# Weight sums for the up projection's Strassen pairs, made in DRAM by accumulating transfers during the mixer

## The chip, the cores and the metric

The kernel runs on one core of one Trainium2 chip. The metric is device time of one execution in microseconds (us), lower is better. Before the change, three runs took 1665.97, 1667.84 and 1670.0 us; the median is 1667.84 us. The engines are TensorE (PE, its weight loads PEld), VectorE (DVE), ScalarE (ACT), GpSimd (POOL) and SyncE (SP). SP and ACT issue nearly all transfers before the change. Each engine works through its own instructions in order and waits for others by semaphores.

## What is computed

One decoder layer on 1024 tokens of width 1024: a mixer (S5 and mLSTM branches, merged by gates), cross-attention into 256 memory tokens, and a gated feed-forward part with a causal convolution over three tokens. What the change touches is the last of these:

```python
def _conv_ffn(h, w_up, conv_w, conv_b, w_down):
    u = _causal_dwconv(h @ w_up, conv_w, conv_b)
    a, b = jnp.split(u, 2, axis=-1)
    return (jax.nn.gelu(a) * b) @ w_down
```

The weight `w_up` is 1024 x 5632 and `h` is 1024 x 1024, all float32.

## The kernel before

**Numbers and tiles.** Weights and activations are split into a high part (float32r) and a low one (the rest), and each product is three matmuls: high by high, high by low, low by high. A tile of a projection (`ntile`, L204) loads 512 KB of weights into a WR buffer from SP, ACT casts them to WH (L176), DVE subtracts to make WL (L177), PE runs 48 matmuls into a PSUM tile M (L202), and DVE drains M. The mixer and the attention consist mainly of such tiles, one after the other, with the small work of the S5 and mLSTM branches between them. The list `ORDER` sets the order of the mixer's parts.

**POOL in the mixer.** It does little: it clears buffers in the S5 part (MEMSET, L484), and it computes powers for normalisations, by `G.tensor_tensor(..., op=ALU.pow)`: L775 for each of the four mLSTM heads (tile `dc`), L230 for the vectors `rm` and `r`. DVE prepares `dc` (L774), POOL takes the power (L775), DVE goes on with it (L776, L779), and then PE transposes the scaled head (L782). L776 stands in DVE's queue behind L774 or a few rows later, so DVE waits there until POOL is done.

**The up projection.** The 44 column blocks of `w_up` form 22 pairs f (`NF` = 22; block f of a with block f of b). Each pair is a 2x2 block product by Winograd's form of Strassen's scheme, with seven products p = 1 to 7 in place of eight. In DRAM, `w_up[f]` is 128 x 2048: quarters 0 to 3 hold a11, a12, a21 and a22, 128 x 512 (256 KB) each. The seven weight operands are a11, a12, a22 and four sums s1 to s4, made by `Pair.load` with four DVE instructions (L1129 to L1132):

```python
V.tensor_tensor(out=s1, in0=a21, in1=a22, op=ALU.add)
V.tensor_tensor(out=s2, in0=s1, in1=a11, op=ALU.subtract)
V.tensor_tensor(out=s3, in0=a11, in1=a21, op=ALU.subtract)
V.tensor_tensor(out=s4, in0=a12, in1=s2, op=ALU.subtract)
```

`Pair.weights(p)` splits one operand into high and low; `Pair.product(p)` (matmuls at L1161) runs 12 matmuls for it and adds the PSUM result to the running sums (L1174, L1178). `Pair.conv` (L1184) applies the convolution, `Pair.finish` the gelu and the product, and sends the result to DRAM (`Gd`).

The list `jobs` sets the order. The first eight pairs (f below `NE` = 8, the early pairs) run their products 1 and 2 during the end of the attention, since these need only the first half of the tokens, and keep the sum (pairs 4 to 7 by way of DRAM, `Cd`). Then come products 6, 7, 5, 4, 3 of pairs 0 to 7, and all seven products of pairs 8 to 21. `weights(k + 7)` is called seven jobs ahead. An early pair's `r0` (a11 and a12) is loaded twice, first for products 1 and 2, and again for the sums.

**Buffers and queues.** The 18 Y buffers (128 x 520) hold quarters, sums and split operands; S, R, Z and VV are buffers of 1024 columns. A transfer into a buffer waits until its last reader is done. SP issues the loads of weights, in order. The scheduler decides the order of each engine's instructions at build time.

Of the kernel before, what the change touches and what calls it, by code (L numbers as in the profile page):

```python
# [19 lines left out]
P = 128  # L20
T = 1024
# [10 lines left out]
NF = DFF // P  # L32
# [51 lines left out]
def hybrid_layer(ctx: ExitStack, tc: tile.TileContext, a):  # L86
    nc = tc.nc
    cp = ctx.enter_context(tc.tile_pool(name="cp", bufs=1))
# [17 lines left out]
    def Z(dt=F32):  # L106
        return sp.tile([P, T], dt, tag="Z", bufs=NZ, name=nm("Z"))

    def Y(dt=F32):
        return Yw(dt)[:, :512]  # L110

    def Yw(dt=F32):
        return sp.tile([P, 520], dt, tag="Y", bufs=NY, name=nm("Y"))
# [4 lines left out]
    def psM():  # L118
        return pm.tile([P, T], F32, tag="M", bufs=2, name=nm("M"))

    def psA():
        return pm.tile([P, 512], F32, tag="A", bufs=4, name=nm("A"))
# [4 lines left out]
    V, A, G, PE = nc.vector, nc.scalar, nc.gpsimd, nc.tensor  # L127
# [6 lines left out]
    def col(name, i=0, n=1):  # L134
        o, _ = COLS[name]
        return cols[:, o + i : o + i + n]
# [22 lines left out]
    pw_ = psA()  # L159
    for _ in range(NWARM):  # L160
        PE.matmul(pw_[:, :P], warm, warm, start=True, stop=True)
# [20 lines left out]
    def load_w(src, shape, alloc=None):  # L182
        fw = shape[0] * shape[1]
        raw = wp.tile([P, T], F32, tag="WR", name=nm("WR"))[:, :fw]
        nc.sync.dma_start(out=raw.rearrange("p (k n) -> p k n", k=shape[0]), in_=src)
        if alloc is None:
            hi = wp.tile([P, T], F32R, tag="WH", name=nm("WH"))[:, :fw]
            lo = wp.tile([P, T], F32R, tag="WL", name=nm("WL"))[:, :fw]
        else:
            hi, lo = alloc(F32R)[:, :fw], alloc(F32R)[:, :fw]  # L190
        wcount[0] += 1
        split(hi, lo, raw, low[wcount[0] % 2])
        return (hi.rearrange("p (k n) -> p k n", k=shape[0]),
                lo.rearrange("p (k n) -> p k n", k=shape[0]))

    def gemm_part(ps, wk, xh, xl, width, first, last):

        wh, wl = wk
        spans = [(s, min(s + 512, width)) for s in range(0, width, 512)]
        for lhsT, rhs, is_first, is_last in ((wh, xh, True, False), (wh, xl, False, False), (wl, xh, False, True)):  # L200
            for s, e in spans:
                PE.matmul(ps[:, s:e], lhsT, rhs[:, s:e], start=first and is_first, stop=last and is_last)  # L202

    def ntile(src, xs, nk=KD, width=T):  # L204

        wh, wl = load_w(src, (nk, P))
        ps = psM()
        for k in range(nk):
            gemm_part(ps, (wh[:, k, :], wl[:, k, :]), xs[k][0], xs[k][1], width, k == 0, k == nk - 1)
        return ps  # L210


    def rstd_col(sq, n, out, more=(), alloc=None):
# [57 lines left out]
    for k in range(KD):  # L271
# [6 lines left out]
        for p_ in parts:  # L278
            w = slice(p_[0].start, p_[-1].stop)
# [4 lines left out]
        for p_ in parts:  # L284
            for w_, x_, f, l in ((wh, xh, True, False), (wh, xl, False, False), (wl, xh, False, True)):
                for j in range(3):
                    for h in p_:
                        PE.matmul(pus[j][h.start // 512], w_[:, 0, j * P : (j + 1) * P], x_[:, h],  # L288
                                  start=k == 0 and f, stop=k == KD - 1 and l)
    r1 = cp.tile([P, 8], F32, name="r1")  # L290
# [125 lines left out]
    for w in (1, 2, 4):  # L416
# [30 lines left out]
                      in_=zt[:, : 4 * 7 * CHG].rearrange("p (x k) -> p x k", x=4))  # L447
# [384 lines left out]
    for step in ORDER:  # L832
        i = int(step[1])
# [23 lines left out]
    for j in range(4):  # L857
        ps = ntile(a["w_glu"][j], ysp, nk=4)
# [52 lines left out]
    for i in range(2):  # L911
# [3 lines left out]
        for k4 in range(4):  # L915
            w = slice(k4 * NM, (k4 + 1) * NM)
# [122 lines left out]
    Gd = dr.tile([NF, P, T], F32, name="Gd")  # L1039
    Cd = dr.tile([4, P, T], F32, name="Cd")  # L1040
    H = H0, H1 = slice(0, 512), slice(512, T)
    r3 = cp.tile([P, 8], F32, name="r3")
    x2sq = Z()
    low[:] = [V, V]
# [12 lines left out]
    def o_tile(half, n):  # L1057
        hs = H[half]
        wh, wl = ow.pop(0)
        ps = psA() if half else psM()[:, H0]  # L1060
        for k in range(KD):
            gemm_part(ps, (wh[:, k, :], wl[:, k, :]), oT[k][0][:, hs], oT[k][1][:, hs], 512, k == 0, k == KD - 1)
        xj = x1[n][:, hs]
        V.tensor_tensor(out=xj, in0=xj, in1=ps, op=ALU.add)
        if n == 0:
            A.activation(out=x2sq[:, hs], in_=xj, func=AF.Square)
        else:
            t = Z()[:, H0]
            A.activation(out=t, in_=xj, func=AF.Square)
            V.tensor_tensor(out=x2sq[:, hs], in0=x2sq[:, hs], in1=t, op=ALU.add)  # L1070
        A.dma_start(out=X2d[n][:, hs], in_=xj)

    def o_norm(half):

        rc = r3[:, 4 * half : 4 * half + 4]
        rstd_col([x2sq[:, H[half]]], D, rc, alloc=psM)
        pb = psM()[:, H0]
# [3 lines left out]
    def normed(n, half, pb):  # L1081
        xj = x1[n][:, H[half]]
        V.scalar_tensor_tensor(out=xj, in0=xj, scalar=col("f_g", n), in1=pb, op0=ALU.mult, op1=ALU.mult)
        return xj
# [5 lines left out]
    def put(p, i, f, alloc):  # L1090
        t = alloc(F32R)
        X[p][i] = hi, lo = t[:, H0], t[:, H1]
        split(hi, lo, f)


    NE, HOLD = 8, 4
    wslot = [6]

    class Pair:
# [9 lines left out]
        def load(self, both):  # L1109

            r0 = wp.tile([P, T], F32, tag="WR", name=nm("WR"))
            nc.sync.dma_start(out=r0, in_=a["w_up"][self.f, :, :T])
            a11, a12 = r0[:, H0], r0[:, H1]
            self.src = {1: a11, 2: a12}
            if not both:
                return
            if HOLD <= self.f < NE:
                self.ra = Z()
                nc.sync.dma_start(out=self.ra, in_=Cd[self.f - HOLD])
            if self.f < NE:  # L1120
                a21, a22 = Y(), Y()
                for i, t in enumerate((a21, a22)):
                    nc.sync.dma_start(out=t, in_=a["w_up"][self.f, :, T + 512 * i : T + 512 * i + 512])
            else:
                r1 = S()
                nc.sync.dma_start(out=r1, in_=a["w_up"][self.f, :, T:])
                a21, a22 = r1[:, H0], r1[:, H1]
            s1, s2, s3, s4 = [Y() for _ in range(4)]
            V.tensor_tensor(out=s1, in0=a21, in1=a22, op=ALU.add)  # L1129
            V.tensor_tensor(out=s2, in0=s1, in1=a11, op=ALU.subtract)  # L1130
            V.tensor_tensor(out=s3, in0=a11, in1=a21, op=ALU.subtract)
            V.tensor_tensor(out=s4, in0=a12, in1=s2, op=ALU.subtract)  # L1132
            self.src = {1: a11, 2: a12, 3: s4, 4: a22, 5: s1, 6: s2, 7: s3}

        def weights(self, p):
# [43 lines left out]

        def conv(self, raw, ct):  # L1180
            acc = S()
            A.activation(out=acc, in_=raw, func=AF.Identity, scale=col("fcw", 3 * ct + 2), bias=col("fcb", ct))  # L1182
            for d_ in range(1, 3):
                V.scalar_tensor_tensor(out=acc[:, d_:], in0=raw[:, : T - d_], scalar=col("fcw", 3 * ct + 2 - d_),  # L1184
                                       in1=acc[:, d_:], op0=ALU.mult, op1=ALU.add)
            return acc

# [94 lines left out]
    t2s = []  # L1282
    for i in range(4):
        xe, xo = x1[2 * i], x1[2 * i + 1]
        b12, b22 = normed(2 * i, 1, pb), normed(2 * i + 1, 1, pb)
        V.tensor_tensor(out=xe[:, H0], in0=b12, in1=xe[:, H0], op=ALU.subtract)
        t2 = Y()
        V.tensor_tensor(out=t2, in0=b22, in1=xe[:, H0], op=ALU.subtract)
        put(6, i, t2, S)
        t2s.append(t2)  # L1290
    for k in range(2 * NE, 2 * NE + 2):
        weights(k)
    for i in range(4):
        xe, xo = x1[2 * i], x1[2 * i + 1]
# [5 lines left out]
        weights(k)  # L1300
    for i in range(4):
        xo = x1[2 * i + 1]
        V.tensor_tensor(out=xo[:, H0], in0=xo[:, H0], in1=t2s[i], op=ALU.subtract)
        put(4, i, xo[:, H0], S)
    for i in range(4):
        put(3, i, x1[2 * i + 1][:, H1], S)
# [25 lines left out]
    last = list(range(NF - 2 * FCH, NF))  # L1332
# [146 lines left out]
def build(shapes):  # L1479
    import concourse.bacc as bacc  # L1480

    nc = bacc.Bacc("TRN2", target_bir_lowering=False, num_devices=1, dynamic_dma_scratch_size=2048)
    a = {}
    for n, s in shapes.items():
        a[n] = nc.dram_tensor(f"in_{n}_dram", s, F32, kind="ExternalInput").ap()
    a["out"] = nc.dram_tensor("out_0_dram", (KD, P, T), F32, kind="ExternalOutput").ap()
    with tile.TileContext(nc, schedule_with_timeline_sim=True) as tc:
        hybrid_layer(tc, a)
    return nc
# [11 lines left out]
```

## Time and profile before

| | before |
|---|---|
| median of three runs | 1667.84 us |
| the profiled execution's span | 1665.3 us |
| TensorE busy in it | 1641.3 us |
| VectorE busy in it | 1102.3 us |
| ScalarE busy in it | 664.2 us |
| GpSimd busy in it | 40.1 us, 50 instructions |
| granted TensorE clock, mean | 0.996 |
| HBM read and written | 130.76 MB, 30.93 MB |

The span of the profiled execution goes from its first to its last instruction. A group of instructions in the profile has the source line, the engine, the operation, the tiles that it writes and reads (without the buffer's number), the count, the total busy time, the mean of one in ns, and the idle time ahead of them with what ended it. The chain is the work that ended last, followed back from the end. The matmuls of the up projection (L1161) start at 975.6 us and end at 1411 us; the mixer lies before some 716 us, the attention between them.

### The profile page before, as it was taken

What the parts mean: (1) busy time and instruction counts of PE and PEld (TensorE: products, weight loads), DVE (VectorE), ACT (ScalarE), POOL (GpSimd) and SP (SyncE); (2) the same over time, 40 slices, a digit from 0 to 9 for tenths busy, and PEclk for the clock granted to TensorE, in tenths of its full rate; (3) what the DMA queues carried; (4) which work ended last, traced back from release to release, by engine and by line L of the source; (5) the groups of instructions that cost most, each with busy time, mean ns of one, the idle gap of its engine ahead of it and who ended that gap; (6) DMA issues with size and microseconds to landing.
All of it is one profiled execution on the core that took longest, in us unless ns stands there. A gap on an engine that the chain in (4) does not pass through costs nothing.

```text
span 1665.3 us, 20759 instructions
## 1 busy us (share of the span) xinstructions
PE 1641.3 (99%) x8139; PEld 1373.8 (82%) x8139; DVE 1102.3 (66%) x1752; ACT 664.2 (40%) x1057; POOL 40.1 (2%) x50
## 2 busy tenths in 40 slices
PE   9999999999999999999999999999999999999997
PEld 7897888888888888888888887877888888888887
DVE  7768767675344344523476569999878977976645
ACT  6446544533332223422354336444444444312113
POOL 0000000000000000000000000000000000000014
PEclk9999999999999999999999999999999999999998
DMA  6231411213211133323133345422222226631102
GB/s 194 91 95 43 118 60 58 53 52 92 73 51 51 45 127 128 126 88 101 64 138 116 108 138 190 135 76 101 89 77 89 89 89 244 210 106 59 52 0 102
DMA packets 62851, 163.04 MB, mean 98 GB/s; under 512 B 6881, under 2 KB 20897, under 8 KB 62753
## 3 DMA queue, kind: packets, MB, share of 16 engines
q1 hardware_dynamic: 55216, 143.19, 26.0%
q10 hardware_dynamic: 7536, 18.53, 3.2%
q8 instruction: 64, 1.05, 0.3%
q14 instruction: 35, 0.28, 0.0%
HBM read 130.76 MB, written 30.93 MB: 97 GB/s over the span
## 4 chain that ended last, share of the span: by engine, by line
PE 84%; DVE 8%; DMA 3%; issue 2%; ACT 2%; SPq 0%; POOL 0%; POOLq 0%; DVEq 0%; ACTq 0%
PE M L202 40%; PE A L1161 9%; PE M L1161 8%; PE M L1328 6%; PE A L1328 6%; PE A L202 3%; PE A L1034 1%; DVE S L1184 1%; PE M L288 1%; DMA Y<-in_w_up_dram 1%; PE A L980 1%; PE A L954 1%; DMA WR<-in_w_up_dram 1%; DVE S L177 1%; DVE W L177 1%
## 5 line engine op out<-in xcount | busy, mean ns | idle before, releaser
L202 PE MATMUL M<-S,WH 128*128 128x512 f32 (+1 forms) x1704 | 460.6, 383 | 1.9 <-DVE R L789 1.4
L202 PEld LDWEIGHTS M<-S,WH 128*128 128x128 f32 x1704 | 314.3, 189 | 63.4 <-issue 2.0
L176 ACT CAST WH<-WR 128x1024 fp32r<-128x1024 f32 (+2 forms) x117 | 109.9, 941 | 426.8 <-PE M L202 258.2
L202 PE MATMUL M<-S,WL 128*128 128x512 f32 (+1 forms) x884 | 278.5, 382 | 0.0
L202 PEld LDWEIGHTS M<-S,WL 128*128 128x128 f32 x884 | 166.4, 189 | 31.4
L177 DVE TENSOR_TENSOR WL<-WR,WH 128x1024 fp32r<-128x1024 f32 (+2 forms) x117 | 126.8, 1084 | 81.2 <-ACT WH L176 76.3
L1161 PE MATMUL M<-S,Y 128*128 128x512 f32 x468 | 115.0, 394 | 0.1
L1161 PEld LDWEIGHTS M<-S,Y 128*128 128x128 f32 x468 | 87.7, 188 | 21.1 <-ACT Y L176 0.6
L1184 DVE SCALAR_TENSOR_TENSOR S<-Z,cols,S 128x1023 f32<-128x1023 f32 (+1 forms) x72 | 90.9, 1280 | 3.7 <-ACT S L1182 3.6
L1161 PE MATMUL M<-S,W 128*128 128x512 f32 x324 | 79.1, 391 | 1.0 <-DVE S L1174 1.0
L789 DVE TENSOR_TENSOR R<-M,R 128x1024 f32<-128x1024 f32 x16 | 19.6, 1222 | 84.0 <-PE M L202 84.0
L1161 PEld LDWEIGHTS M<-S,W 128*128 128x128 f32 x324 | 60.6, 188 | 14.8 <-DVE S L1174 1.4
L1161 PE MATMUL A<-S,W 128*128 128x512 f32 x288 | 70.8, 391 | 1.5 <-ACT W L176 1.5
L176 ACT CAST W<-Y 128x512 fp32r<-128x512 f32 x51 | 31.4, 619 | 89.2 <-PE A L1161 67.1
L1161 PEld LDWEIGHTS A<-S,W 128*128 128x128 f32 x288 | 53.9, 188 | 14.0 <-ACT W L176 2.3
L1161 PE MATMUL A<-S,Y 128*128 128x512 f32 x240 | 61.0, 394 | 0.0
L1161 PE MATMUL A<-R,W 128*128 128x512 f32 x228 | 56.4, 391 | 0.0
L1161 PE MATMUL A<-VV,W 128*128 128x512 f32 x216 | 54.7, 395 | 0.0
L1161 PEld LDWEIGHTS A<-S,Y 128*128 128x128 f32 x240 | 45.1, 188 | 10.6
L202 PE MATMUL A<-S,WH 128*128 128x512 f32 (+1 forms) x184 | 53.1, 371 | 0.5 <-ACT WH L176 0.5
L1161 PEld LDWEIGHTS A<-R,W 128*128 128x128 f32 x228 | 42.7, 188 | 9.4 <-ACT Z L1168 0.2
L1182 ACT ACTIVATE S<-Z,cols 128x1024 f32<-128x1024 f32 x36 | 43.2, 1238 | 15.9 <-DVE Z L1178 13.4
(463 smaller groups left out, 3032.2 us busy)
## 6 DMA issues: line engine op xcount, KB each, us to landing
WR<-in_w_up_dram SPq DMA_DIRECT2D x30, 512.0 KB, 3.9
WR<-in_w_in_dram SPq DMA_DIRECT2D x29, 512.0 KB, 3.4
Gd<-S SPq DMA_DIRECT2D x22, 512.0 KB, 2.7
WR<-in_w_down_dram SPq DMA_DIRECT2D x22, 512.0 KB, 3.4
Z<-Gd SPq DMA_DIRECT2D x20, 512.0 KB, 5.2
WR<-in_w_o_dram SPq DMA_DIRECT2D x16, 512.0 KB, 3.4
S<-in_w_up_dram SPq DMA_DIRECT2D x14, 512.0 KB, 3.8
Y<-Rd SPq DMA_DIRECT2D x16, 256.0 KB, 5.2
```

The lines of the kernel that those rows point to most:

```text
L176: A.copy(out=hi, in_=src)
L177: (lo_eng or V).tensor_tensor(out=lo, in0=src, in1=hi.bitcast(F32), op=ALU.subtract)
L202: PE.matmul(ps[:, s:e], lhsT, rhs[:, s:e], start=first and is_first, stop=last and is_last)
L288: PE.matmul(pus[j][h.start // 512], w_[:, 0, j * P : (j + 1) * P], x_[:, h], start=k == 0 and f, stop=k == KD - 1 and l)
L789: V.tensor_tensor(out=gt, in0=ps, in1=rb, op=ALU.mult)
L954: PE.matmul(pv[2 * m + j], lhsT, rhs[:, 0, 512 * j : 512 * j + 512], start=k == 0 and f, stop=k == KD - 1 and l)
L980: PE.matmul(ps[:, i * NM : (i + 1) * NM], lhsT[:, tok], rhs, start=f, stop=l)
L1034: PE.matmul(po, lhsT[:, ns], rhs, start=f, stop=l)
L1161: PE.matmul(ps, lhsT[:, c], rhs, start=f, stop=l, skip_group_check=True)
L1182: A.activation(out=acc, in_=raw, func=AF.Identity, scale=col("fcw", 3 * ct + 2), bias=col("fcb", ct))
L1184: V.scalar_tensor_tensor(out=acc[:, d_:], in0=raw[:, : T - d_], scalar=col("fcw", 3 * ct + 2 - d_), in1=acc[:, d_:], op0=ALU.mult, op1=ALU ...
L1328: PE.matmul(ps[h], lhsT[:, 0, cs_], rhs[:, w], start=f, stop=l)
```

## The change

**New in the mixer.** A DRAM tile `Ws` of 22 x 4 x 128 x 512 (23 MB) holds the four sums of each pair. Each call of `ntile` ends with a call of `up_sums`. After the 2nd, 8th, 14th and so on to the 62nd tile, 11 times, it issues a batch for two pairs from POOL's queue: four copies from `w_up` to `Ws`, the first of which waits for the tile's last matmul, and four accumulating transfers, which add a quarter or another sum to what stands in `Ws`. Each transfer is 512 KB (two pairs, 256 KB each). An accumulate waits for the landing of those that it builds on.

**Only additions.** The four sums are now q2+q3, q0+q2+q3, q0+q2 and q0+q1+q2+q3. The signs that this turns are taken up in the sums of activations (L1286, L1288, L1303) and in the second half's convolution weights (`nfcw`, the negative of the weights in `cols`).

**In the up projection.** `Pair.load` no longer computes sums. It loads s2, s3, s1 and s4 from `Ws` and a22 from `w_up` into five Y buffers. The quarter a21 isn't loaded any more. `r0` is still loaded a second time for the early pairs, with no reader.

```diff
-                PE.matmul(ps[:, s:e], lhsT, rhs[:, s:e], start=first and is_first, stop=last and is_last)
+                last_mm[0] = PE.matmul(ps[:, s:e], lhsT, rhs[:, s:e], start=first and is_first, stop=last and is_last)
...
+SUM_FROM, SUM_STEP = 2, 6
...
+        up_sums()
         return ps
+
+    Ws = dr.tile([NF, 4, P, 512], F32, name="Ws")
+    SB = 2
+    tiles_done = [0]
+
+    def up_sums():
+        tiles_done[0] += 1
+        b, off = divmod(tiles_done[0] - SUM_FROM, SUM_STEP)
+        if off or not 0 <= b < NF // SB:
+            return
+        fs = slice(SB * b, SB * b + SB)
...
+        for i, q in ((0, 2), (1, 0), (2, 0), (3, 1)):
+            d = nc.gpsimd.dma_start(out=o(i), in_=w(q))
+            tc.add_manual_dep(d.ins, last_mm[0].ins.name, DependencyInfo(DependencyClass.Sync, DependencyReason.DATA), reason="pace")
+        nc.gpsimd.dma_start(out=o(0), in_=w(3), accum_op=ALU.add)
+        nc.gpsimd.dma_start(out=o(1), in_=w(2), accum_op=ALU.add)
+        nc.gpsimd.dma_start(out=o(2), in_=o(0), accum_op=ALU.add)
+        nc.gpsimd.dma_start(out=o(3), in_=o(2), accum_op=ALU.add)
...
+    nfcw = cp.tile([P, 3 * NF], F32, name="nfcw")
+    V.tensor_scalar_mul(nfcw, col("fcw", 3 * NF, 3 * NF), -1.0)
...
-            if self.f < NE:
-                a21, a22 = Y(), Y()
-                for i, t in enumerate((a21, a22)):
-                    nc.sync.dma_start(out=t, in_=a["w_up"][self.f, :, T + 512 * i : T + 512 * i + 512])
-            else:
-                r1 = S()
-                nc.sync.dma_start(out=r1, in_=a["w_up"][self.f, :, T:])
-                a21, a22 = r1[:, H0], r1[:, H1]
-            s1, s2, s3, s4 = [Y() for _ in range(4)]
-            V.tensor_tensor(out=s1, in0=a21, in1=a22, op=ALU.add)
-            V.tensor_tensor(out=s2, in0=s1, in1=a11, op=ALU.subtract)
-            V.tensor_tensor(out=s3, in0=a11, in1=a21, op=ALU.subtract)
-            V.tensor_tensor(out=s4, in0=a12, in1=s2, op=ALU.subtract)
+            a22, s1, s2, s3, s4 = [Y() for _ in range(5)]
+            for t, i in ((s2, 2), (s3, 1), (s1, 0), (s4, 3)):
+                nc.sync.dma_start(out=t, in_=Ws[self.f, i])
+                if i == 0:
+                    nc.sync.dma_start(out=a22, in_=a["w_up"][self.f, :, T + 512 :])
```

**Where POOL's instructions stand.** POOL's queue around the powers of heads 1, 2 and 3, before (L775 is the power on `dc`, one row for each head; L484 clears a buffer of the S5 part; the brackets name the engines whose semaphores a row waits for):

```order
L775 TENSOR_TENSOR dc_2205<-dc_2205,mhalf 128x8 [waits DVE_49]
L775 TENSOR_TENSOR dc_2528<-dc_2528,mhalf 128x8 [waits DVE_49,Activation_49,Pool_49]
L484 MEMSET Y_2622 128x256 [waits DVE_49,PE_49]
L775 TENSOR_TENSOR dc_2927<-dc_2927,mhalf 128x8 [waits DVE_49,Activation_49,Pool_49]
L230 TENSOR_TENSOR rm<-ms_5714,mhalf 128x2 [waits DVE_49]
```

The same place after the change (L807 is the power, L516 the clearing; L237 are the copies, L239 to L242 the accumulates, DMASW the landings of POOL's own transfers):

```order
L807 TENSOR_TENSOR dc_2214<-dc_2214,mhalf 128x8 [waits DVE_49]
L807 TENSOR_TENSOR dc_2545<-dc_2545,mhalf 128x8 [waits DVE_49,Activation_49,Pool_49]
L516 MEMSET Y_2639 128x256 [waits DVE_49,PE_49]
L237 DMA Ws<-in_w_up_dram 128x2x512 [waits PE_49]
L237 DMA Ws<-in_w_up_dram 128x2x512 x3
L239 DMA Ws<-in_w_up_dram 128x2x512 [waits DMASW0_49]
L240 DMA Ws<-in_w_up_dram 128x2x512 [waits DMASW5_49,DMASW1_49]
L241 DMA Ws<-Ws 128x2x512 [waits DMASW4_49,DMASW2_49]
L242 DMA Ws<-Ws 128x2x512 [waits DMASW7_49,DMASW6_49,DMASW3_49]
L807 TENSOR_TENSOR dc_2944<-dc_2944,mhalf 128x8 [waits DVE_49,Activation_49,Pool_49]
```

The batch of tile 14 now stands ahead of head 3's power, and with it three steps that each wait for a landing. In the same way tile 8's batch stands ahead of head 1's power, tile 2's ahead of head 0's (with one L516 among its accumulates), and tile 56's ahead of `rm`. DVE's row behind the power (L776 before, L808 after) and its wait for POOL stay where they were.

**Where SP's loads stand.** SP's queue from the first early pair's load, before (L1112 is `r0` into WR, L1123 a quarter into Y):

```order
L1123 DMA Y_8160<-in_w_up_dram 128x512 [waits DMAHW4_49,PE_49]
L1123 DMA Y_8161<-in_w_up_dram 128x512 [waits PE_49]
L1112 DMA WR_8158<-in_w_up_dram 128x1024 [waits DMAHW3_49,DVE_49]
L1112 DMA WR_8217<-in_w_up_dram 128x1024 [waits DMAHW7_49,DMAHW2_49,DVE_49]
L1123 DMA Y_8219<-in_w_up_dram 128x512 [waits DVE_49]
L1123 DMA Y_8220<-in_w_up_dram 128x512 [waits DVE_49]
```

The same place after the change (L1161 is a sum from `Ws`, L1163 is a22, L1151 is `r0`):

```order
L1161 DMA Y_8252<-Ws 128x512 [waits DMASW4_49,PE_49]
L1151 DMA WR_8249<-in_w_up_dram 128x1024 [waits DMAHW7_49,DMAHW3_49,DVE_49]
L1163 DMA Y_8251<-in_w_up_dram 128x512 [waits PE_49,Pool_49]
L1161 DMA Y_8255<-Ws 128x512 [waits DMASW7_49,PE_49]
L1151 DMA WR_8306<-in_w_up_dram 128x1024 [waits DMAHW2_49,DVE_49]
L1151 DMA WR_8418<-in_w_up_dram 128x1024 [waits DMAHW7_49]
L1151 DMA WR_8526<-in_w_up_dram 128x1024 [waits DMAHW4_49,DMAHW2_49]
L1151 DMA WR_8634<-in_w_up_dram 128x1024 [waits DMAHW5_49,DMAHW3_49]
L1151 DMA WR_8745<-in_w_up_dram 128x1024 [waits DMAHW6_49,DMAHW4_49]
L1161 DMA Y_8310<-Ws 128x512 [waits PE_49]
```

Before, pair 1's two quarters (Y_8219, Y_8220) follow pair 0's loads after two loads of WR. Now five loads of WR stand between pair 0's last sum and pair 1's first one; four of them wait for landings of other transfers and for no engine.

More of the change, by code (lines that the diff above doesn't have):

```diff
@@ L7 @@
 from concourse import mybir
+from concourse.mybir import DependencyClass, DependencyInfo, DependencyReason
 from concourse._compat import with_exitstack
@@ L201, in gemm_part @@
             for s, e in spans:
-                PE.matmul(ps[:, s:e], lhsT, rhs[:, s:e], start=first and is_first, stop=last and is_last)
+                last_mm[0] = PE.matmul(ps[:, s:e], lhsT, rhs[:, s:e], start=first and is_first, stop=last and is_last)
+    last_mm = [None]
     def ntile(src, xs, nk=KD, width=T):
@@ L209, in ntile, with w, o @@
             gemm_part(ps, (wh[:, k, :], wl[:, k, :]), xs[k][0], xs[k][1], width, k == 0, k == nk - 1)
+        up_sums()
         return ps
+    Ws = dr.tile([NF, 4, P, 512], F32, name="Ws")
[7 more added lines that the diff above has]
+        fs = slice(SB * b, SB * b + SB)
+        def w(i):
+            return a["w_up"][fs, :, 512 * i : 512 * i + 512].rearrange("f p c -> p f c")
+        def o(i):
+            return Ws[fs, i].rearrange("f p c -> p f c")
+        for i, q in ((0, 2), (1, 0), (2, 0), (3, 1)):
[5 more added lines that the diff above has]
+        nc.gpsimd.dma_start(out=o(3), in_=o(2), accum_op=ALU.add)
     def rstd_col(sq, n, out, more=(), alloc=None):
@@ L1041, in hybrid_layer, with fcw @@
     H = H0, H1 = slice(0, 512), slice(512, T)
+    nfcw = cp.tile([P, 3 * NF], F32, name="nfcw")
+    V.tensor_scalar_mul(nfcw, col("fcw", 3 * NF, 3 * NF), -1.0)
+    def fcw(ct, d_):
+        i = 3 * ct + 2 - d_
+        return col("fcw", i) if ct < NF else nfcw[:, i - 3 * NF : i - 3 * NF + 1]
     r3 = cp.tile([P, 8], F32, name="r3")
@@ L1181, in conv @@
             acc = S()
-            A.activation(out=acc, in_=raw, func=AF.Identity, scale=col("fcw", 3 * ct + 2), bias=col("fcb", ct))
+            A.activation(out=acc, in_=raw, func=AF.Identity, scale=fcw(ct, 0), bias=col("fcb", ct))
             for d_ in range(1, 3):
-                V.scalar_tensor_tensor(out=acc[:, d_:], in0=raw[:, : T - d_], scalar=col("fcw", 3 * ct + 2 - d_),
+                V.scalar_tensor_tensor(out=acc[:, d_:], in0=raw[:, : T - d_], scalar=fcw(ct, d_),
                                        in1=acc[:, d_:], op0=ALU.mult, op1=ALU.add)
@@ L1285, in hybrid_layer @@
         b12, b22 = normed(2 * i, 1, pb), normed(2 * i + 1, 1, pb)
-        V.tensor_tensor(out=xe[:, H0], in0=b12, in1=xe[:, H0], op=ALU.subtract)
+        V.tensor_tensor(out=xe[:, H0], in0=xe[:, H0], in1=b12, op=ALU.subtract)
         t2 = Y()
-        V.tensor_tensor(out=t2, in0=b22, in1=xe[:, H0], op=ALU.subtract)
+        V.scalar_tensor_tensor(out=t2, in0=b22, scalar=-1.0, in1=xe[:, H0], op0=ALU.mult, op1=ALU.subtract)
         put(6, i, t2, S)
@@ L1302, in hybrid_layer @@
         xo = x1[2 * i + 1]
-        V.tensor_tensor(out=xo[:, H0], in0=xo[:, H0], in1=t2s[i], op=ALU.subtract)
+        V.scalar_tensor_tensor(out=xo[:, H0], in0=t2s[i], scalar=-1.0, in1=xo[:, H0], op0=ALU.mult, op1=ALU.subtract)
         put(4, i, xo[:, H0], S)
```

## The prediction

> **What bounds the kernel now.** I read the page's head and its chain first, then windows of 50 us over the up projection, then the groups of that stretch, then the lanes of POOL, DVE and PE around the places where the new transfers are put.
>
> ```profile
> span 1665.3 us, 20759 instructions
> PE 1641.3 (99%) x8139; PEld 1373.8 (82%) x8139; DVE 1102.3 (66%) x1752; ACT 664.2 (40%) x1057; POOL 40.1 (2%) x50
> ...
> GB/s 194 91 95 43 118 60 58 53 52 92 73 51 51 45 127 128 126 88 101 64 138 116 108 138 190 135 76 101 89 77 89 89 89 244 210 106 59 52 0 102
> ...
> PE 84%; DVE 8%; DMA 3%; issue 2%; ACT 2%; SPq 0%; POOL 0%; POOLq 0%; DVEq 0%; ACTq 0%
> ```
>
> TensorE is busy 99% of the span and carries 84% of the chain of work that ended last. No DVE time is worth anything by itself, then; it pays only where DVE paces TensorE. The page's share can't show that place; the windows can (time stretch, length, then busy us and count of PE, PEld, DVE, ACT, POOL, the granted clock, and the DMA share and rate):
>
> ```profile
> 500.00:550.00 50.00, 50.00 (x221) 41.14 (x220) 22.79 (x32) 12.51 (x17) 0.00 (x0) 1.00 0.16 48
> ...
> 1025.00:1075.00 50.00, 49.29 (x215) 39.89 (x214) 46.25 (x67) 20.18 (x28) 0.00 (x0) 1.00 0.48 154
> 1075.00:1125.00 50.00, 48.27 (x209) 38.71 (x208) 47.05 (x62) 22.33 (x27) 0.00 (x0) 1.00 0.25 86
> 1125.00:1175.00 50.00, 49.87 (x215) 40.04 (x215) 45.98 (x61) 24.02 (x35) 0.00 (x0) 1.00 0.31 106
> 1175.00:1225.00 50.00, 50.00 (x219) 40.76 (x218) 45.17 (x61) 22.21 (x32) 0.00 (x0) 1.00 0.24 84
> 1225.00:1275.00 50.00, 50.00 (x218) 40.73 (x217) 40.16 (x56) 21.99 (x33) 0.00 (x0) 1.00 0.24 85
> 1275.00:1325.00 50.00, 50.00 (x219) 40.75 (x219) 40.19 (x53) 21.52 (x30) 0.00 (x0) 1.00 0.22 74
> 1325.00:1375.00 50.00, 50.00 (x218) 40.75 (x217) 39.76 (x56) 20.56 (x31) 0.00 (x0) 1.00 0.28 95
> ```
>
> In the mixer 221 matmuls fill 50 us. In the up projection the later pairs run 218 or 219, and from 1025 to 1175 us, most of it the eight early pairs (f below NE), only 215, 209 and 215, with DVE busy 46 to 47 of 50 us. There DVE is what TensorE waits for. The chain over that stretch agrees (start, length, what):
>
> ```profile
> 1028.54 5.40 DMA Y<-in_w_up_dram
> ...
> 1042.79 0.70 DVE Y L1129
> ...
> 1045.33 0.69 DVE Y L1132
> ...
> 1073.20 5.66 DMA Y<-in_w_up_dram
> ```
>
> A quarter of the weights lands, and then the sums that the change takes away stand on the path (the first and the last of four are shown), 0.7 us each.
>
> **What is removed.** The sums, by group in the stretch 976 to 1413 us (count, total busy us and mean ns of one, idle time ahead of them):
>
> ```profile
> L1132 DVE TENSOR_TENSOR Y<-WR,Y 128x512 f32<-128x512 f32 x22 | 15.2, 690 | 0.0
> L1130 DVE TENSOR_TENSOR Y<-Y,WR 128x512 f32<-128x512 f32 x22 | 15.2, 689 | 0.1
> L1131 DVE TENSOR_TENSOR Y<-WR,S 128x512 f32<-128x512 f32 x14 | 9.6, 689 | 0.0
> L1129 DVE TENSOR_TENSOR Y<-S 128x512 f32<-128x512 f32 x14 | 9.6, 688 | 3.9 <-DMA S<-in_w_up_dram 3.9
> L1129 DVE TENSOR_TENSOR Y<-Y,Y 128x512 f32<-128x512 f32 x8 | 5.5, 693 | 5.1 <-DMA Y<-in_w_up_dram 5.1
> L1131 DVE TENSOR_TENSOR Y<-WR,Y 128x512 f32<-128x512 f32 x8 | 5.5, 689 | 0.0
> ```
>
> That is 88 instructions and 15.2+15.2+9.6+9.6+5.5+5.5 = 60.6 us of DVE. An early pair has 5 products of 12 matmuls, 60 in all, at 50/218.5 = 0.229 us: 13.7 us of TensorE. The 150 us from 1025 hold 639 matmuls, 10.6 such pairs' worth, with 139.3 us of DVE, so 13.1 us of DVE for 60 matmuls, and that with its waits for landings is what paces it; four sums are 2.8 us of it. Without them DVE has 10.3 us against 13.7, and TensorE should set the pace. The later pairs (84 matmuls) are already at the rate that is left to have, so their 56 sums bring nothing: TensorE hides them.
>
> The gain is what those 150 us lack: 3 x 218.5 - (215+209+215) = 16.5 matmuls of 0.229 us, **3.8 us**. Its low end is PE's idle time alone, 0.71+1.73+0.13 = 2.6 us. Its high end counts the seven windows from 1025 to 1375 against the mixer's 221: 1547 - 1513 = 34 matmuls at 50/221 = 0.226 us, 7.7 us; I don't expect the later pairs to reach that, as PE shows no idle time there.
>
> The subtractions whose signs are turned (L1286, L1288, L1303) stay instructions of one kind and size on the same engine, and nfcw is one DVE instruction of 128x66 near the kernel's start: nothing, hidden by PE.
>
> **What is added on SP.** An early pair loads 5 quarters of 256 KB in place of 2, a later one 1.25 MB in place of 0.5 MB. At 0.22 to 0.48 of the DMA share there is room. The price is in time to landing (KB each, median us):
>
> ```profile
> Z<-Gd SPq DMA_DIRECT2D x20, 512.0 KB, 5.2
> WR<-in_w_up_dram SPq DMA_DIRECT2D x30, 512.0 KB, 3.9
> Gd<-S SPq DMA_DIRECT2D x22, 512.0 KB, 2.7
> Y<-in_w_up_dram SPq DMA_DIRECT2D x16, 256.0 KB, 4.5
> ```
>
> Five loads of WR (SP rows 210 to 214 after) now stand ahead of pair 1's sums, each waiting for a landing: 5 x 3.9 = 19.5 us at most, against the 13.7 us of pair 0's products behind which they run. So the cost lies between 0 and 5.8 us, once. I take 0: loads of WR may be out long before pair 0 begins.
>
> **What is added on POOL.** 88 transfers, 8 in a batch. Each batch holds the in-order queue from its tile's last matmul until its last accumulate is issued. Call that X. The trace has no transfer issued by POOL, none from DRAM to DRAM and no accumulating one. From below: three landings that follow one another (a copy, an accumulate, the third accumulate) at the 2.7 us of the write to Gd, 8 us. From above: seven transfers, none beside another, at the 7.0 us of this row, 49 us:
>
> ```profile
> S<-X1d SPq DMA_DIRECT2D x8, 512.0 KB, 7.0
> ```
>
> By rate, 4 copies and 3 accumulates are 7 x 0.524 = 3.7 MB; at the page's best slice, 244 GB/s, 15 us; if an accumulate costs two transfers, since it must also read its target, 10 x 0.524 MB give 21.5 us. I take **18 us**, between the two. The Trainium skill, page "DMA: Bandwidth & Descriptors", section "Anatomy of one DMA — SWDGE (gpsimd) path", fits a transfer issued by GpSimd as about 2.0 us and bytes over 436 GB/s. By it 512 KB take an estimated 3.2 us and three in a row 9.6 us, so X would be near my lower end; no run here shows it, and the 3.9 and 5.2 us landings above are slower than it.
>
> What X can hide behind is in these rows, of POOL, then DVE, PE and ACT:
>
> ```profile
> 327.47 1.64 POOL L775 TENSOR_TENSOR dc<-dc,mhalf 128x8 f32<-128x8 f32 x1 [36.91 <-DVE dc L774]
> 716.24 0.69 POOL L230 TENSOR_TENSOR rm<-ms,mhalf 128x2 f32<-128x2 f32 x1 [387.14 <-DVE ms L229]
> ...
> 133.75 1.21 DVE L685 TENSOR_TENSOR R<-M,R 128x1024 f32<-128x1024 f32 x1
> 219.41 1.22 DVE L685 TENSOR_TENSOR R<-M,R 128x1024 f32<-128x1024 f32 x1
> 246.31 0.17 DVE L776 TENSOR_TENSOR dc<-dc 128x8 f32<-128x8 f32 x1 [1.75 <-POOL dc L775]
> 307.43 1.22 DVE L789 TENSOR_TENSOR R<-M,R 128x1024 f32<-128x1024 f32 x1
> 330.41 0.16 DVE L776 TENSOR_TENSOR dc<-dc 128x8 f32<-128x8 f32 x1
> 330.60 1.29 DVE L779 TENSOR_TENSOR Y<-Y,dc 128x512 f32<-128x512 f32 x2
> 682.61 1.29 DVE L885 TENSOR_TENSOR S<-S,M 128x512 f32<-128x512 f32 x2 [6.15 <-PE M L202]
> 332.85 1.03 PE L782 MATMUL A<-ident,Y 128*128 128x128 f32 x8
> 146.62 1.01 ACT L488 COPY Y<-S 64x64 f32<-64x64 f32 x4
> ```
>
> The DVE rows with M are the drains of tiles 2, 8, 14 and 56, whose last matmuls release a batch. Tile 14's batch stands ahead of head 3's dc on POOL: released by 307.43, wanted by DVE at 330.41 less the 1.64 us it takes, so DVE is held from X = 21.3 us, and PE, whose transposes start at 332.85 when DVE ends at 331.9, from 22.3. Tile 8's batch is ahead of head 1's dc: 246.31 - 1.64 - 219.41 gives 25.3 us. Tile 2's holds a MEMSET for two copies' landing (8.6 us for all four at 244 GB/s), against 146.62 - 133.75 = 12.9 us. The one ahead of rm has 716.24 - 682.61 = 33.6 us. Behind a late dc stand DVE's drains of M and the splits of weights, all of them in order, so what is late there is late for PE. With X = 18 us all are covered, and the term is 0.
>
> **The sum.** The span of 1665.3 us lies 2.5 us under the median of 1667.84. The sum against the span is 1665.3 - 3.8 = 1661.5 us, and with the 2.5 us kept, 1664.0 us.
>
> **The rivals.** *The landings take the sums' place* (B). The chain has two quarters' landings of 5.4 and 5.7 us in the early pairs, and now the sums themselves must land in Y buffers that come free no sooner. PE's missing 3.8 us would stay: 1667.8. Against it: the loads no longer wait for anything of DVE's work on the same pair, and four DVE passes behind each landing are gone.
>
> *POOL is held too long* (C), the slower one. Its place is head 3's dc, its threshold X = 22.3 us. At 30 us PE loses 7.7 us there and 30 - 25.3 = 4.7 at head 1: 1664.0 + 12.4 = 1676.4. At 35 us it is 12.7 + 9.7 + 1.4 at rm: 1687.8. For it: my 18 us are only 4 under the threshold, and if accumulates cost two transfers 1 us is left. Another way into it: if POOL could issue only while DVE rests, then with an issue as long as POOL's 1.64 us row, seven are 11.5 us, and this stretch leaves DVE 22.4 of 50 us, so that they stretch to 26 us:
>
> ```profile
> 300.00:350.00 50.00, 48.59 (x299) 40.87 (x299) 27.60 (x57) 24.59 (x50) 1.64 (x1) 1.00 0.18 51
> ```
>
> The Trainium skill has such a rule on the page "SBUF — State Buffer", section "SBUF: two separate sides": while DVE runs an operation in a two-port mode, GpSimd can't write the descriptors of its transfers. No run here shows it. Against it speaks that DVE's work there is in short pieces.
>
> *The removal reaches nothing* (D): the early pairs are short for want of something other than DVE, such as the drain of products. Also 1667.8.
>
> **How the numbers follow.** A measurement of this kernel tells 0.2%, 3.3 us, from no change. My case has 0.55: its gain of 2.6 to 7.7 us is over 3.3 us in 0.37 and under it in 0.18. B and D together have 0.13, 0.11 of it no change and 0.02 slower. C has 0.32: at 23 to 29 us of X, gain and loss cancel (0.05); beyond that it is slower (0.27). Faster 0.37, same 0.34, slower 0.29. The range goes from 1660 (the 7.7 us) to 1687 (X of 35 us), and leaves out the longest holds. The likeliest case's own range is 1660 to 1666.
>
> **What would show it.** Right: the windows over the early pairs hold some 218 matmuls, DVE's total is some 60 us shorter, the waits of DVE for POOL's dc stay at 1.75 us, and POOL's row for head 3 stays within 22 us of tile 14's drain. C shows as DVE waiting many us for POOL's dc at heads 1 and 3, with PE idle behind it near 220 to 340 us; B as PE or ACT waiting for Y<-Ws. Wrong altogether: PE loses time in the mixer where no dc waits, by loads of weights that land late beside the batches, which I priced at nothing because casts to WH wait 258.2 us in all, 59 times, for PE rather than for weights:
>
> ```profile
> L176 ACT CAST WH<-WR 128x1024 fp32r<-128x1024 f32 (+2 forms) x117 | 109.9, 941 | 426.8 <-PE M L202 258.2
> ```

## The result and the profile after

The changed kernel takes 1685.8 us (median of four runs, 1684.13 to 1687.99) against 1668.05 us of the kernel before in the same comparison: ratio 1.0106, 95% interval 1.0092 to 1.0119. It is 1% slower, where 1664.0 us and a gain were forecast. The ratios in this document are estimates over all runs of a comparison and can differ by up to 0.001 from the quotient of two medians. The head of its page:

```profile
span 1684.8 us, 21115 instructions
PE 1648.7 (98%) x8139; PEld 1380.7 (82%) x8139; DVE 1053.9 (63%) x1665; ACT 664.7 (39%) x1057; POOL 122.1 (7%) x138
...
PE 73%; DMA 3%; issue 2%; DVE 2%; POOL 1%; ACT 0%; SPq 0%; POOLq 0%; DVEq 0%; ACTq 0%
```

The removal did what it says: DVE is busy for 48.4 us less (1102.3 to 1053.9) with 87 instructions less. The shares of the chain can't be compared with those of the kernel before, since this chain goes back only to 326.9 us; in the changed kernel's second profile, whose chain reaches the start, DVE has 3% in place of 8%. The span grew by 19.5 us all the same. Some rows of POOL serve as clocks, since they follow TensorE's progress (the two from 309 us on are the first issue of tile 14's batch and head 3's power behind it):

```profile
211.33 1.68 POOL L807 TENSOR_TENSOR dc<-dc,mhalf 128x8 f32<-128x8 f32 x1 [52.77 <-DVE dc L806]
277.30 1.64 POOL L807 TENSOR_TENSOR dc<-dc,mhalf 128x8 f32<-128x8 f32 x1 [29.22 <-DVE dc L806]
309.47 2.84 POOL L237 DMA_DIRECT2D Ws<-in_w_up_dram  x4 [17.17 <-PE M L204]
332.86 2.12 POOL L807 TENSOR_TENSOR dc<-dc,mhalf 128x8 f32<-128x8 f32 x1
727.95 0.71 POOL L262 TENSOR_TENSOR rm<-ms,mhalf 128x2 f32<-128x2 f32 x1 [6.21 <-DVE ms L261]
996.32 1.01 POOL L262 TENSOR_TENSOR r<-ms,mhalf 128x4 f32<-128x4 f32 x1 [41.03 <-DVE ms L261]
```

The same rows of the kernel before start at:

```profile
209.55 1.64 POOL L775 TENSOR_TENSOR dc<-dc,mhalf 128x8 f32<-128x8 f32 x1 [85.77 <-DVE dc L774]
275.51 1.64 POOL L775 TENSOR_TENSOR dc<-dc,mhalf 128x8 f32<-128x8 f32 x1 [29.23 <-DVE dc L774]
...
984.70 1.01 POOL L230 TENSOR_TENSOR r<-ms,mhalf 128x4 f32<-128x4 f32 x1 [41.26 <-DVE ms L229]
```

So the lag is 1.8 us at 210 and at 277 us, 11.7 at `rm` (716.24 before), 11.6 at 985, and 19.5 at the end of the span. Some 10 us are lost between 277 and 716, nothing in the attention, 8 net after it. Starts of TensorE's matmuls with the same number in both traces put it closer (times of the changed kernel): +10.0 us between 334 and 425, +9.0 between 1025 and 1060, -3.1 between 1080 and 1190, +1.8 between 1400 and 1460. The windows of the changed kernel there:

```profile
300.00:350.00 50.00, 47.41 (x293) 39.36 (x292) 27.77 (x59) 23.75 (x52) 9.15 (x9) 1.00 0.56 134
350.00:400.00 50.00, 44.42 (x236) 37.29 (x234) 30.45 (x52) 15.17 (x20) 7.61 (x8) 0.95 0.54 142
1000.00:1050.00 50.00, 42.14 (x179) 33.78 (x178) 38.38 (x62) 26.96 (x51) 0.00 (x0) 0.93 0.68 224
1050.00:1100.00 50.00, 50.00 (x219) 40.81 (x219) 37.06 (x48) 21.26 (x28) 0.00 (x0) 1.00 0.57 181
1100.00:1150.00 50.00, 50.00 (x220) 41.05 (x219) 44.47 (x58) 23.81 (x31) 0.00 (x0) 1.00 0.40 132
```

The early pairs now run 219 and 220 matmuls per 50 us, at the later pairs' rate, with PE busy throughout. The losses stand beside them: 5.6 us of idle PE from 350 to 400, 7.9 from 1000 to 1050, and at both places a granted clock under 1. TensorE's waits in the two stretches (who waited for whom, total, times, longest):

```profile
PE A L603 <- DMA Z<-Kd: 3.0, 1, 3.0
PE A L567 <- DMA Z<-Ud: 2.6, 1, 2.6
PE M L204 <- DVE R L821: 1.4, 1, 1.4
PE A L814 <- DVE Y L811: 1.2, 1, 1.2
...
PE A L1192 <- ACT W L178: 7.9, 1, 7.9
```

The 1.4 us for R stood in the kernel before as well. The 1.2 are head 3's late power. New and larger are two loads of the last S5 part, Ud and Kd. The transfers issued from 365 to 402 us (KB, median us to landing):

```profile
Ws<-in_w_up_dram POOLq DMA_DIRECT2D x6, 512.0 KB, 10.0
Ws<-Ws POOLq DMA_DIRECT2D x2, 512.0 KB, 6.9
WR<-in_w_in_dram SPq DMA_DIRECT2D x1, 512.0 KB, 10.4
Z<-Ud SPq DMA_DIRECT2D x1, 512.0 KB, 18.0
Z<-Kd SPq DMA_DIRECT2D x8, 64.0 KB, 9.3
```

In the kernel before, the same loads from 362 to 398 us:

```profile
Z<-Ud SPq DMA_DIRECT2D x1, 512.0 KB, 4.8
Z<-Kd SPq DMA_DIRECT2D x8, 64.0 KB, 2.6
```

Batch 3 issues its four copies at 372.98 us and Z<-Ud goes out at 375.4, into the same 16 engines: 18.0 us in place of 4.8, and the chain holds the whole of it. What TensorE paid for it after the wait is seen in windows of 5 us (the last three numbers are the clock, the DMA share and the rate):

```profile
384.00:389.00 5.00, 5.00 (x24) 4.14 (x23) 3.02 (x6) 2.78 (x4) 0.00 (x0) 1.00 1.10 233
389.00:394.00 5.00, 2.41 (x17) 1.78 (x17) 1.81 (x3) 0.03 (x1) 1.28 (x1) 1.00 1.11 276
394.00:399.00 5.00, 2.06 (x28) 1.66 (x24) 3.32 (x6) 0.00 (x0) 0.23 (x1) 0.58 0.67 149
399.00:404.00 5.00, 4.95 (x14) 4.11 (x15) 0.36 (x1) 0.73 (x1) 0.91 (x1) 0.50 0.64 105
404.00:409.00 5.00, 5.00 (x21) 4.07 (x20) 4.88 (x11) 2.75 (x3) 0.00 (x0) 0.89 0.08 14
```

Behind the idle time the granted clock drops to half, and it stays there for some 10 us: from 399 to 404 us PE is busy and does 14 matmuls where 24 fit at full clock. A stall of 5.6 us, two waits with 32 short matmuls between them, thus cost about 8.6: the lag grows from 3.2 us at 380 to 11.7 at 410.

The second stall, in SP's lane (start, length, engine) and then in the chain:

```profile
1018.38 9.49 SPq L1151 DMA_DIRECT2D WR<-in_w_up_dram  x5
1027.92 1.77 SPq L1161 DMA_DIRECT2D Y<-Ws  x3
...
1028.73 8.69 DMA Y<-Ws
...
1039.23 10.53 PE A L1192 x36
```

Five dead loads of `r0`, each held for the landing of another, occupy SP for 9.5 us; pair 1's first sums go out at 1027.92, land in 8.7 us, and TensorE, out of work at 1031, starts again at 1039.23.

### The profile page after: what moved, and what is told of

Read it like the earlier page. It is cut to its first block, busy times and chain, and to the rows that moved or that the text cites. A ratio compares the mean times of both kernels' runs of the same rounds, so it can differ in the third digit from the quotient of the medians.

```text
span 1684.8 us, 21115 instructions
## 1 busy us (share of the span) xinstructions
PE 1648.7 (98%) x8139; PEld 1380.7 (82%) x8139; DVE 1053.9 (63%) x1665; ACT 664.7 (39%) x1057; POOL 122.1 (7%) x138
## 4 chain that ended last, share of the span: by engine, by line
PE 73%; DMA 3%; issue 2%; DVE 2%; POOL 1%; ACT 0%; SPq 0%; POOLq 0%; DVEq 0%; ACTq 0%
PE M L204 30%; PE A L1192 14%; PE M L1192 10%; PE M L1359 5%; PE A L1359 5%; PE A L204 3%; PE A L1066 1%; PE A L1012 1%; DMA Z<-Ud 1%; PE A L986 1%; POOL S L1435 1%; DMA Y<-Ws 1%; DMA Gd<-S 0%; DMA S<-Gd 0%; PE A L1053 0%
## 5 line engine op out<-in xcount | busy, mean ns | idle before, releaser
L178 ACT CAST WH<-WR 128x1024 fp32r<-128x1024 f32 (+2 forms) x117 | 110.0, 941 | 437.5 <-PE M L204 260.3
L1215 DVE SCALAR_TENSOR_TENSOR S<-Z,cols,S 128x1023 f32<-128x1023 f32 (+1 forms) x44 | 56.2, 1278 | 6.2 <-ACT S L1213 6.1
L1417 POOL TENSOR_TENSOR Z<-Z,Y 128x512 f32<-128x512 f32 x7 | 9.1, 1298 | 644.3 <-ACT Y L1413 643.8
```

The lines of the kernel that those rows point to most:

```text
L178: A.copy(out=hi, in_=src)
L1417: (G if si < 1 else V).tensor_tensor(out=sq[:, :nt], in0=sq[:, :nt], in1=t, op=ALU.add)
```

## The experiments

**The batches moved behind the S5 parts (e1_late).**

```diff
-SUM_FROM, SUM_STEP = 2, 6
+SUM_FROM, SUM_STEP = 22, 4
```

> The eleven batches start after tile 22 and follow every 4th tile (22, 26, ... 62), so that none runs before the last S5 part has loaded its Ud and Kd; the up projection is as in the changed kernel. Theory: the 10 us that the changed kernel loses against the one before between 335 and 425 us come from batch 2 ahead of head 3's power (some 1.4 us) and from batch 3's transfers, which make Z<-Ud land in 18.0 us in place of 4.8 (5.6 us of idle TensorE and then 10.2 us at half clock). Then Z<-Ud lands in about 5 us again, the time is about 10 us below the changed kernel's, 1675 to 1677 us, and the stall of 7.9 us near 1031 us is still there. Rival: any batch beside the mixer's tiles costs, wherever it stands (weights that land late); then closer batches cost as much or more, and the time stays at 1684 to 1690 us.

1679.83 us, ratio to the kernel before 1.006 (1.0045 to 1.0075). Z<-Ud lands in 4.8 us, and TensorE's waits for Ud and head 3 are gone; at 700 us the lag is 1.7 us in place of 11.7. But the time missed the forecast by 3 us, for a new place of the same kind: the batch after tile 58 now stands ahead of `rm`.

```profile
706.73 2.78 POOL L237 DMA_DIRECT2D Ws<-in_w_up_dram  x4 [16.69 <-PE M L204]
...
723.73 1.14 POOL L241 DMA_DIRECT2D Ws<-Ws  x1 [7.39 <-DMA Ws<-in_w_up_dram]
724.44 1.18 POOL L262 TENSOR_TENSOR rm<-ms,mhalf 128x2 f32<-128x2 f32 x1
```

TensorE waits 3.8 us for `rm` in this kernel. The queue's hold on a power is real, then, and its price depends on where it falls.

**Batches 0 to 2 left, the others moved.**

```diff
-SUM_FROM, SUM_STEP = 2, 6
+SUM_AT = [2, 8, 14, 24, 29, 34, 39, 44, 49, 54, 59]
```

> Batches 0 to 2 stay after tiles 2, 8 and 14; batches 3 to 10 go to tiles 24, 29, ... 59. Theory: only head 3's late power is left in the mixer, 1 to 2 us over the kernel with all batches late, so 1676 to 1679 us, and Z<-Ud lands in about 5 us. Rival: the late power itself, which delays DVE by some 4 us, brings about what follows at 390 us; then the time stays at 1682 to 1686 us and L567 still waits.

1676.87 us, ratio 1.0049 (1.0034 to 1.0064), inside the forecast. L814 still waits 1.4 us for head 3, Z<-Ud lands in 4.6 us, and no wait for Ud or Kd over 0.2 us is left. The late power alone costs 1.6 us between 300 and 360 us and brings nothing in its train, as the theory said.

**The dead loads left out.**

```diff
-            r0 = wp.tile([P, T], F32, tag="WR", name=nm("WR"))
-            nc.sync.dma_start(out=r0, in_=a["w_up"][self.f, :, :T])
+            if not both or self.f >= NE:
+                r0 = wp.tile([P, T], F32, tag="WR", name=nm("WR"))
+                nc.sync.dma_start(out=r0, in_=a["w_up"][self.f, :, :T])
```

> The early pairs' second load of r0, which nothing reads any more, is left out; the batches are as in the changed kernel. Theory: five of these loads, each behind the landing of another, hold SP from 1018.4 to 1027.9 us, ahead of pair 1's sums; without them the 7.9 us of idle TensorE near 1031 us and the 6.8 us at half clock behind it (3.4 us) go, and the three us won later stay: about 11 us less than the changed kernel, 1673 to 1676 us. Rival: the landing of Y<-Ws itself (8.7 us in the chain) is what TensorE waits for, or the Y buffers come free too late; then the wait stays at over 4 us and the time at 1680 us or more.

1675.24 us, ratio 1.0043 (1.0029 to 1.0058), inside the forecast. The wait of 7.9 us falls to 1.0. SP's lane shows why:

```profile
1015.61 3.35 SPq L1153 DMA_DIRECT2D WR<-in_w_up_dram  x2
1019.97 1.98 SPq L1163 DMA_DIRECT2D Y<-Ws  x3
```

The same load goes out 8 us sooner. The mixer's loss is untouched (Z<-Ud 17.6 us), so the two are separate.

**Both edits.**

> Both edits: late batches and no dead loads. Theory: the two losses are separate and add, so some 21 us less than the changed kernel, 1662 to 1667 us, about 3 us or a little more under the kernel before. Rival: the early pairs are held by something else than DVE's sums and nothing is won there; then 1667 to 1670 us.

1670.2 us, ratio 1.001 (1.0001 to 1.002). The losses add as the theory says: alone the two edits win 6.0 and 10.6 us, together 15.6. But the time stays 3 us over the range given, next to the rival's, and no gain shows, though the rival's reason doesn't hold: the profile shows 3.0 us won in the early pairs. `rm` waits 0.5 us here, at the same schedule as in the first experiment, so that price varies with the landings.

**The batches alone, without their use.** The kernel before, with `up_sums` and its calls added, and with DVE's sums kept.

> The kernel before with the eleven batches of the changed kernel added and nothing else: the sums are still made by DVE, nobody reads Ws. Theory: this costs what the changed kernel lost in the mixer, 10 us, by head 3's late power and Z<-Ud's late landing with the half clock behind it: 1675 to 1680 us, and TensorE waits for Z<-Ud and Z<-Kd again. Rival: the mixer's loss needs the changed order or the nfcw instruction; then 1668 to 1671 us.

1675.88 us, ratio 1.0051 (1.0037 to 1.0065), inside the forecast. The mixer's loss comes whole, with neither the new order of the up projection nor `nfcw`:

```profile
PE A L603 <- DMA Z<-Kd: 3.9, 1, 3.9
PE A L567 <- DMA Z<-Ud: 2.0, 1, 2.0
PE M L204 <- DVE R L821: 1.4, 1, 1.4
PE A L814 <- DVE Y L811: 1.2, 1, 1.2
```

**Clear of rm as well (e6_apart).** No dead loads, and:

```diff
-SUM_FROM, SUM_STEP = 2, 6
+SUM_AT = [24, 28, 32, 36, 40, 44, 48, 52, 56, 60, 64]
```

> No dead loads, and the batches after tiles 24, 28, ... 56, 60 and 64, so that none starts in the 34 us ahead of rm either (in e1_late the one after tile 58 kept rm and with it TensorE waiting for 3.8 us). Theory: the wait for rm goes and the three us in the early pairs stay: 1666 to 1669 us, no more than 1 us from the kernel before. Rival: batches beside the attention's loads cost there; then 1670 us or more.

1668.5 us, ratio 1.0006 (0.9998 to 1.0014): as the kernel before. The losses named so far are gone, but a small one is new, of the kind that the rival names. Beside the batch after tile 64, which starts at 759.14 us, four loads of weights of the attention land in 6.0 us (median; 3.2 in the kernel before), and TensorE waits for a cast:

```profile
WR<-in_w_vv_dram SPq DMA_DIRECT2D x4, 512.0 KB, 6.0
...
PE M L204 <- ACT WH L178: 0.5, 1, 0.5
```

The lag grows by 1.0 us there (1.8 and 1.1 us in the two other kernels below with these batches). Of the 3.1 us won in the early pairs this explains a part; the rest must have been lost elsewhere.

**nfcw made later.** The one instruction gets a dependence on the last matmul emitted before it.

> As e6_apart, with nfcw made behind the first part of the program in place of DVE's sixth row. Theory: nfcw's wait for its columns costs nothing, and the 1 to 2 us that the changed kernel lies behind in its first 70 us are chance of that execution (the half clock at 60 us): within 1 us of e6_apart. Rival: it is nfcw that starts the late half clock; then 1 to 2 us less than e6_apart and no half clock near 60 us.

1669.26 us, ratio 1.0011 (1.0002 to 1.0019), within 1 us of the last. The lag in the first 70 us stays, so it isn't `nfcw`.

**Sums that cost nothing.** No batches and no dead loads; in place of each sum, a quarter of `w_up`, so that this kernel leaves the sums out of its result but keeps the loads in their place:

```diff
-                nc.sync.dma_start(out=t, in_=Ws[self.f, i])
+                nc.sync.dma_start(out=t, in_=a["w_up"][self.f, :, 512 * i : 512 * i + 512])
```

> No batches at all; where the changed kernel loads a sum from Ws, this one loads a quarter of w_up of the same size, so that the sums are left out of the computation. No dead loads. This is what the removal of DVE's sums is worth when the sums cost nothing. Theory: the early pairs give back 3 us as in the changed kernel, and some 1.5 us are lost again at the change to the down projection: 1665 to 1668 us. Rival: it is batches left over in the attention that hide a larger gain; then 1660 to 1664 us.

1667.19 us against 1667.22, ratio 0.9996 (0.9987 to 1.0006). This is the key run: even sums for free, with the loads kept, are worth nothing that can be measured; by the interval the gain is at most 0.13%, 2.2 us. Its windows, and TensorE's longest wait in the last of them:

```profile
1050.00:1100.00 50.00, 50.00 (x219) 40.83 (x218) 45.03 (x56) 22.91 (x29) 0.00 (x0) 1.00 0.47 148
1100.00:1150.00 50.00, 50.00 (x219) 40.91 (x219) 43.64 (x54) 25.24 (x32) 0.00 (x0) 1.00 0.39 126
...
1400.00:1450.00 50.00, 48.59 (x213) 39.28 (x212) 45.80 (x54) 19.84 (x20) 0.00 (x0) 1.00 0.72 253
...
PE M L1360 <- DVE WL L179: 1.3, 1, 1.3
```

The early pairs run at full rate, 3.0 us won against the first profile of the kernel before. But at the change to the down projection PE is idle for 1.4 us, 1.3 of them for a WL of DVE, where the kernel before has 50.00 of 50 us busy with 221 matmuls, and 2.0 us go back.

**Only the early pairs from Ws.** Four batches, after tiles 24, 28, 32 and 36; from pair 8 on, DVE's four sums as before, as additions; no dead loads.

> Only the early pairs take their sums from Ws: four batches, after tiles 24, 28, 32 and 36; the later pairs load a21 and a22 into S and sum on DVE as before, with additions. No dead loads. Theory: the early pairs give back 3 us, the attention and the change to the down projection stay as they were before, so nothing is given back: 1664 to 1666 us, faster than both kernels. Rival: the 1.5 to 2 us at the change to the down projection come from the early pairs' lead itself, or the gain is lost on the later pairs; then 1666 to 1668 us.

1667.25 us against 1667.55, ratio 0.9993 (0.9984 to 1.0002). The give-back at 1400 to 1450 us shrinks to some 0.9 us, yet the time isn't clearly below the kernel before: the forecast was missed, the rival's range held it.

**The first loads for the down projection sooner.** As the kernel with tiles 24 to 64, with one line moved:

```diff
-        if jobs[k] == (NF - 1, 1):
+        if jobs[k] == (NF - 2, 4):
             nxt = hidden(chunks[0], S), load_down(chunks[0], None)
+        if jobs[k] == (NF - 1, 1):
```

> As e6_apart, with the first chunk's loads for the down projection (two of Gd and two of w_down) emitted six jobs sooner, ahead of pair 20's product 4. Theory: the loss of 1.5 to 2.5 us at the change to the down projection comes from ACT's cast of S<-Gd, which waits 5 us for its load and holds the convolution and then DVE's WL behind it; sooner loads take it away: 1666 to 1667.5 us. Rival: it comes from DVE's own order; then as e6_apart, 1668 to 1669 us.

1668.5 us, ratio 0.9999 (0.999 to 1.0008): nothing won, and in the rival's range. The first wait, for WL, is gone, but others stand in its place, so that the late cast of S<-Gd isn't the cause, or not alone:

```profile
PE A L1362 <- DVE R L1364: 1.0, 1, 1.0
PE M L1194 <- DVE Z L1207: 0.3, 1, 0.3
```

**Second profiles of both kernels.**

> The kernel before, unchanged, for a second profile: if the half clock near 60 us, which all variants show and the first profile of the kernel before doesn't, is chance of an execution, it may show it, with some 1.5 to 3 us more in the first 70 us; if it belongs to the change it doesn't. 1665 to 1670 us.

1665.23 us. The dip of the clock at 60 us is there this time:

```profile
60.00:65.00 5.00, 5.00 (x33) 5.00 (x33) 5.00 (x12) 0.63 (x2) 0.00 (x0) 0.73 0.75 243
```

So the 1.8 us at the start of the changed kernel's profile need not come from the change; in its second profile, below, the same matmuls even start 0.2 us sooner than in the first one of the kernel before. This profile also loses less in the early pairs than the first one, 0.8 us by the starts of the same matmuls, which leaves 2.2 to 3.1 us for the removal of the sums.

> The changed kernel, unchanged, for a second profile: Z<-Ud lands in 15 to 20 us again and TensorE waits 7 to 8 us for pair 1's first sum again, if these are what sets its time; 1683 to 1688 us. If they were chance of the first profile, one of them is gone while the time stays.

1681.57 us, 1.4 us under the range given. Both stalls come again (Z<-Ud in 17.6 us):

```profile
PE A L1192 <- ACT W L178: 7.2, 1, 7.2
PE A L567 <- DMA Z<-Ud: 2.2, 1, 2.2
PE A L603 <- DMA Z<-Kd: 2.0, 1, 2.0
```

## Why the prediction was wrong, step by step

- *What bounds the kernel, and the gain of 3.8 us* (range 2.6 to 7.7): the place and the mechanism were right. The early pairs went from 209 to 215 matmuls per 50 us to 219 and 220, and 3.1 us were won there, 2.2 against the second profile, a little under the range. One reading was off: the 60.6 us of DVE add up rows that overlap (L1130 starts at 1043.52 us and lasts 0.69, L1131 starts at 1044.13). DVE's busy time fell by 48.4 us, 2.2 in place of 2.8 for the four sums of a pair, which still leaves DVE, with 10.9 us, under the 13.7 of TensorE.
- *The later pairs' sums bring nothing*: right; their rate stays at 219.
- *X, 18 us*: too small. Batch 2 started at 309.47 us and freed POOL for the power at 332.86, 23.4 us; batch 1 took some 24. The copies landed in 8.4 us (median) and the accumulates from `w_up` in 10.6 and 11.0, far above the 3.2 us estimated beside the sum. The threshold of 22.3 us was right: 1.1 us over it, 1.2 us of wait at head 3, and none at head 1, whose threshold was 25.3. Rival C's mechanism was there, but was worth 1.6 us. Its other way, a POOL that issues only while DVE rests, isn't seen: with DVE busy 27.8 of the 50 us from 300, the four copies of batch 2 took 2.84 us to issue, 0.7 each.
- *Loads that land late beside the batches, priced at nothing*: the first step that failed. The prediction named a loss of this kind as what would show it wrong, but it looked at the loads of weights, which do have slack in the changed kernel: casts to WH wait 260.3 us for PE, 258.2 before, and from 425 to 970 us, with later batches running, the lag stays at 11.7 to 11.8 us. The last S5 part's loads of Ud and Kd go out where they are needed, and with batch 3 beside them they landed in 18.0 us in place of 4.8: 5.6 us of idle TensorE. Moving the batch away takes it back, and the batches alone bring it.
- *Five loads of WR ahead of pair 1's sums, 0 to 5.8 us, taken as 0*: the second step that failed, with its upper end too low. It counted five landings against pair 0's products, and left out that the sums must land behind them (8.7 us, where 4.5 was the row at hand): TensorE waited 7.9 us. Without the dead loads 1.0 us is left.
- *The granted clock*: the sum had no term for it, the third gap. In the profile before it is 1.00 over the whole mixer. Each of the two stalls dropped it to half, and the mixer's cost 10 us for 6.3 us of new waiting (1.2 + 2.6 + 3.0, less the 0.5 that the kernel before waits for Kd), that of the up projection 9 for 7.9.
- *Nothing is late next*: the sum let the 3.8 us stand to the end. The run with free sums shows 2.0 of its 3.0 us given back at the change to the down projection, where TensorE then waits for DVE. Which of DVE's or ACT's instructions there sets it stays open: sooner loads moved the wait and didn't remove it.
- *The rivals and the range*: D is out, as the removal reached the early pairs. B shows once, at pair 1's first sum, and not in the pairs behind it. The range's upper end, 1687 us, came from a hold of POOL of 35 us; that the measured 1685.8 lies under it is luck, since the hold was 23 to 25 us and the loss came by other ways.

Against the span of 1665.3 us: 1.8 at the start (chance, as far as the second profiles show), 10.0 in the mixer, 9.0 ahead of pair 1, 3.1 won in the early pairs, 1.8 given back, 1684.8 in all. No version was measured that beats the kernel before; the best, with sums for the early pairs alone, has a ratio of 0.9993 (0.9984 to 1.0002).

## What to carry to other kernels

Before work is moved to transfers, list every load in that stretch that is issued shortly before its use and reckon what its landing becomes with the engines full; average DMA share and slack of the weight loads say nothing of it. When data that an engine used to compute arrives by transfer, look what stands ahead of it in the issuing queue, and delete loads whose reader is gone. And try the removal with the replacement left out first: here that one run says that the idea, with its loads kept, had at most 2.2 us to win.

## What the runs showed of the hardware that wasn't expected

A stall of TensorE costs more than its length: behind the two waits of 2.6 and 3.0 us the clock was 0.50 from 399 to 404 us, and behind the one of 7.9 us 0.66 from 1040 to 1045. Where a stall is gone, so is the dip: with the batches late (e1_late) the clock is 1.00 from 385 to 410 us, and with both edits it is 1.00 from 1000 to 1050. The Trainium skill describes this on the page "TensorE: Matmul & The Clock Gate", section "Part 1: The HAM clock gate": a free-running window of about 3.4 us, after an idle one of which the clock is halved. The stall of 7.9 us agrees. The waits of 2.6 and 3.0 us, with 32 matmuls between them, are each shorter than that window, and the clock fell all the same. Nor is the wait's length enough to tell: the dip at 60 us follows a wait of only 2.4 us, which both profiles of the kernel before have and only the second answers with a lower clock (0.73 from 60 to 65 us).

The copies from DRAM to DRAM were slower than any group of this size before: 512 KB in 8.4 us (median) for copies, four at a time (4.6 to 12.8), against medians of 2.7 to 7.0 us between DRAM and SBUF. An accumulate that followed with no other of POOL's transfers beside it, Ws on Ws, took 6.3 us. The issue of one held POOL for 0.7 us, copy or accumulate: an accumulate's row is 1.1 to 1.2 us long, but POOL's power at 332.86 us starts 0.71 behind the start of the accumulate ahead of it.
